# Earlier splits of transposed activations, a decay branch on ScalarE and a square summed by TensorE in a two-layer encoder

## The chip, the cores and the metric

The kernel runs on one NeuronCore of a Trainium2 chip. It is written in Python on a tile framework: each call becomes one instruction of an engine, and a scheduler sets the order of the instructions on each engine from the order in which they are written and from priorities. TensorE (PE; its weight loads are shown as PEld) multiplies, VectorE (DVE), ScalarE (ACT) and GpSimd (POOL) work elementwise, and SyncE's queue (SP) issues the transfers. Each engine takes its own instructions strictly in order. The metric is the device time of one execution in microseconds (us), the median over runs.

## The reference

The input is x, 512 tokens by 1024 features, float32. The trunk has two layers, each with a token mixer and a channel mixer, and each of these four stages is normalised before and after (a "sandwich"):

```python
for layer in range(DEPTH):                                   # DEPTH = 2
    hn = rms_norm(x, norm_mix_pre[layer])
    m = retention_na_mixer(hn, ...) if layer % 2 == 0 else ssd_mixer(hn, ...)
    x = x + rms_norm(m, norm_mix_post[layer])
    f = conv_geglu_ffn(rms_norm(x, norm_ffn_pre[layer]), ...)
    x = x + rms_norm(f, norm_ffn_post[layer])
```

The state space mixer (ssd_mixer) of the second layer is where two of the three edits are:

```python
proj = hn @ w_in                                             # z, x, B, C, dt
xbc = silu(depthwise_conv_centered(xbc, conv_w, conv_b))     # width 5
log_a = dt * A                                               # both directions
y = bidir_scan(C, B, xh * dt_f, xh * dt_b, log_a_f, log_a_b) # 4 groups of 8 heads, chunks of 128
y = (y + xh * d_skip) * silu(z)
yg = y * rsqrt(mean(y * y over the 512 features of a group) + EPS)
return (yg * norm_g) @ w_out
```

Within a chunk of the scan, position j takes from position l the product of C and B times a decay exp(cs_j - cs_l), where cs is the running sum of log_a: for l before j that of the forward direction, for l after j that of the backward one. The channel mixer is `u = conv3(hn @ w_up); (gelu(gate) * val) @ w_down` with 2816 inner features.

## The kernel before, in words

**Arithmetic.** Every large product is made of three matmuls (`mm3`, L84 to L88): a float32 operand is split into a rounded part "hi" and a rest "lo", and hi·hi (L86), lo·hi (L87) and hi·lo (L88) are summed in PSUM. `split` (L79) is two instructions, a cast on ACT (L81) that makes hi and a subtraction on DVE (L82) that makes lo. Weights arrive in units of 128 x 1024 (`wunit`: tile wst by DMA, then whi and wlo); activations are split as xh and xl (normalised input of a stage), yh and yl (output of the state space layer), hh and hl (inner features of the channel mixer).

**Between two stages** each of the four token tiles t goes through one chain: the last matmul of the tile gives m; mg = m·gain (L150); ACT sums the squares of m (junk, L119); v_m (DVE, L109) and r_m (POOL, L111) are the inverse root; x is updated in two halves (`post_norm`, L175); ACT sums the squares of x; v_x and r_x follow; xs, the normalised x, is made in two halves (`norm`, L131); PE transposes xs into pt (`turn`, L140); and `split` makes xh and xl of pt. Only then can the next stage multiply that tile. The splits of weights stand at `high_priority(60)`; that of `turn` has no raised priority. Tiles t2 and t3 at the end of a mixer are "late": their transposes are put between the first products of the next stage (`flush`). The channel mixer makes its first two feature tiles in two column halves, first the 256 columns of t0 and t1, then those of t2 and t3; the weights of the second feature tile go into buffers hh and hl of the channel mixer's own pool.

**The state space layer** works through 4 groups of 8 heads, by the order lists `SLOTS` (a letter each: t and n project a feature tile, h makes the decay matrix of a head, s a state, i the part between chunks, p a pair of heads, r the norm, o the output product of the group before, S and N the silus). `head` (from L730) fetches two rows broadcast over the partitions (pb[0] and pb[1], of 3 buffers, issued by SP), and for each of 4 chunks makes one branch with ACT (L741), takes the maximum with the other by one DVE instruction (L742), and makes ds with ACT (L744); then come an exponential on ACT (L745) and two products on DVE (L746, L747). `inter` starts y with x·d (L768, L769) and adds the parts between chunks. `pair` multiplies (py, L782), adds and gates (L785, L786), and takes the square sq on ACT (L788); POOL adds the squares of pairs 1 to 3 to that of pair 0 (L792), and then yh and yl are made (L794, L795). `rms` (L798) sums the added squares over partitions with four matmuls of one column (pss, L802), and DVE (ss, L804) and POOL (rg, L806) make the inverse root. After group 3 follows its output product with weights whi, wlo and wo, m (L828), and the chain between the stages.

## Time and profile before

| | before |
|---|---|
| median of 3 runs | 1434.11 us (1434.01 to 1434.52) |
| the profiled execution's own time | 1435.78 us |
| its span, first to last instruction | 1434.0 us |
| mean granted TensorE clock | 0.996 of full speed |
| PE busy | 1398.5 us (98%) |
| DVE busy | 946.3 us (66%) |
| ACT busy | 720.3 us (50%) |
| POOL busy | 60.6 us (4%) |

The profile is one execution taken by the hardware profiler. The table's shares are means over four stages: mixer 0, the first channel mixer, the state space layer (from about 620 us to about 1060 us), and the second channel mixer. An engine with a low mean can be full in one of them. The chain that ended last is made of PE for 80% of the span, of DVE for 9%, of ACT for 5%, and of transfers for 3%.

### The profile page before, as it was taken

How to read it: one execution, taken by the hardware profiler on the slowest of the kernel's cores; microseconds unless marked ns; L12 is line 12 of the kernel's file. 1: busy time of each engine (PE TensorE's matmuls, PEld its weight loads, DVE VectorE, ACT ScalarE, POOL GpSimd, SP SyncE). 2: the span in 40 equal slices, each digit the busy share in tenths (PEclk: the TensorE clock that was granted, in tenths of full speed). 3: DMA queues.
4: the chain of work that ended last, by engine and by line, in shares of the span. 5: the costliest groups of instructions: out<-in, count | busy, mean ns of one | idle time of the engine just before them, and what ended most of it. 6: DMA issues, size and time to landing. Idle time of an engine off the chain costs nothing.

```text
span 1434.0 us, 18009 instructions
## 1 busy us (share of the span) xinstructions
PE 1398.5 (98%) x6832; PEld 1141.0 (80%) x6832; DVE 946.3 (66%) x1486; ACT 720.3 (50%) x1192; POOL 60.6 (4%) x67
## 2 busy tenths in 40 slices
PE   7999999999999999999999999999889999999998
PEld 6877777898888888888777787777678888888886
DVE  7368888666566552357889786999886666564242
ACT  5356665454444431334888766577544444443230
POOL 0010110100000000000000000000110000000000
PEclk9999999999999999999999999999999999999999
DMA  7443232233233333332556354345432233333241
GB/s 255 146 141 92 85 96 77 83 108 102 89 98 95 102 94 97 120 107 95 159 180 184 111 176 131 95 153 162 143 120 87 90 100 94 100 89 102 89 132 59
DMA packets 56950, 166.34 MB, mean 116 GB/s; under 512 B 7200, under 2 KB 7968, under 8 KB 56864
## 3 DMA queue, kind: packets, MB, share of 16 engines
q1 hardware_dynamic: 56864, 165.20, 37.2%
q8 instruction: 54, 0.88, 0.2%
q14 instruction: 32, 0.26, 0.1%
HBM read 157.57 MB, written 5.51 MB: 114 GB/s over the span
## 4 chain that ended last, share of the span: by engine, by line
PE 80%; DVE 9%; ACT 5%; DMA 3%; issue 2%; POOL 0%; SPq 0%; DVEq 0%; POOLq 0%; ACTq 0%
PE mm L86 24%; PE mm L87 24%; PE mm L88 24%; DMA pb<-pd 1%; DVE wlo L82 1%; PE st L719 1%; DVE xf L683 1%; PE pt L140 1%; PE y L449 1%; PE pi L762 1%; DMA wst<-in_c_out 1%; PE pt L663 1%; PE py L782 1%; DVE ti L766 1%; DVE yl L795 0%
## 5 line engine op out<-in xcount | busy, mean ns | idle before, releaser
L88 PE MATMUL mm<-xl,whi 128*128 128x512 f32 (+2 forms) x1216 | 463.9, 382 | 4.0 <-DVE xl L82 3.8
L86 PE MATMUL mm<-xh,whi 128*128 128x512 f32 (+2 forms) x1216 | 464.0, 382 | 1.5 <-ACT z L689 0.7
L87 PE MATMUL mm<-xh,wlo 128*128 128x512 f32 (+2 forms) x1216 | 463.4, 381 | 1.4 <-DVE wlo L82 1.4
L82 DVE TENSOR_TENSOR wlo<-wst,whi 128x1024 fp32r<-128x1024 f32 (+1 forms) x208 | 255.5, 1229 | 198.0 <-ACT whi L81 195.8
L81 ACT CAST whi<-wst 128x1024 fp32r<-128x1024 f32 (+1 forms) x208 | 217.3, 1045 | 191.4 <-PE mm L87 119.6
L88 PEld LDWEIGHTS mm<-xl,whi 128*128 128x128 f32 (+1 forms) x1216 | 228.6, 188 | 48.4 <-DVE xl L82 4.5
L86 PEld LDWEIGHTS mm<-xh,whi 128*128 128x128 f32 (+1 forms) x1216 | 229.0, 188 | 46.8 <-issue 2.4
L87 PEld LDWEIGHTS mm<-xh,wlo 128*128 128x128 f32 (+1 forms) x1216 | 229.0, 188 | 45.2 <-DVE wlo L82 2.7
L227 DVE SCALAR_TENSOR_TENSOR cv<-mm,cwt,cv 128x511 f32<-128x511 f32 x88 | 65.7, 747 | 95.2 <-ACT cv L226 94.9
L86 PE MATMUL mm<-whi,hh 128*128 128x512 f32 x288 | 112.0, 389 | 0.0
L87 PE MATMUL mm<-whi,hl 128*128 128x512 f32 x288 | 112.0, 389 | 0.0
L88 PE MATMUL mm<-wlo,hh 128*128 128x512 f32 x288 | 112.0, 389 | 0.0
L226 ACT ACTIVATE cv<-mm,cwt 128x512 f32<-128x512 f32 x88 | 68.4, 777 | 39.8 <-PE mm L88 39.8
L81 ACT CAST hh<-cv 128x512 fp32r<-128x512 f32 x44 | 27.3, 621 | 100.5 <-DVE cv L235 100.3
L233 ACT ACTIVATE cv<-cv 128x512 f32<-128x512 f32 x44 | 27.8, 633 | 85.2 <-DVE cv L228 85.2
L228 DVE SCALAR_TENSOR_TENSOR cv<-mm,cwt,cv 128x511 f32<-128x511 f32 x88 | 66.0, 750 | 3.0
L744 ACT ACTIVATE ds<-um,tok,ddt 128x128 f32<-128x128 f32 x128 | 55.7, 484 | 16.1 <-DVE e L747 15.7
L88 PEld LDWEIGHTS mm<-wlo,hh 128*128 128x128 f32 x288 | 54.1, 188 | 11.3
L87 PEld LDWEIGHTS mm<-whi,hl 128*128 128x128 f32 x288 | 54.1, 188 | 11.2
L86 PEld LDWEIGHTS mm<-whi,hh 128*128 128x128 f32 x288 | 54.1, 188 | 11.2
L82 DVE TENSOR_TENSOR hl<-cv,hh 128x512 fp32r<-128x512 f32 x44 | 30.5, 693 | 28.9 <-ACT hh L81 28.9
L741 ACT ACTIVATE e<-pb,tok 128x128 f32<-128x128 f32 x128 | 43.0, 392 | 11.7 <-DMA pb<-pd 10.2
(236 smaller groups left out, 1945.6 us busy)
## 6 DMA issues: line engine op xcount, KB each, us to landing
wst<-in_f_up SPq DMA_DIRECT2D x88, 512.0 KB
wst<-in_f_down SPq DMA_DIRECT2D x44, 512.0 KB
wst<-in_c_fm SPq DMA_DIRECT2D x40, 512.0 KB
pb<-pd SPq DMA_DIRECT2D x64, 256.0 KB
wst<-in_ab_fm SPq DMA_DIRECT2D x20, 512.0 KB
gain<-yd SPq DMA_DIRECT2D x32, 256.0 KB
wst<-in_c_out SPq DMA_DIRECT2D x16, 512.0 KB
gain<-in_norms SPq DMA_DIRECT2D x8, 512.0 KB
```

Source lines behind the costliest of these rows:

```text
L81: self.nc.scalar.copy(hi, src)
L82: self.nc.vector.tensor_tensor(lo, src, hi.bitcast(F32), op=ALU.subtract)
L86: mm(out, lh, rh, start=first, stop=False)
L87: mm(out, ll, rh, start=False, stop=False)
L88: mm(out, lh, rl, start=False, stop=last)
L140: nc.tensor.transpose(pt[:, j], xs[:, j * P:(j + 1) * P], self.ident)
L226: nc.scalar.activation(o, ps, AF.Identity, scale=w(1), bias=w(3))
L227: nc.vector.scalar_tensor_tensor(o[:, 1:], ps[:, :S - 1], w(0), o[:, 1:], op0=ALU.mult, op1=ALU.add)
L228: nc.vector.scalar_tensor_tensor(o[:, :S - 1], ps[:, 1:], w(2), o[:, :S - 1], op0=ALU.mult, op1=ALU.add)
L233: nc.scalar.activation(g, g, AF.Gelu_apprx_tanh)
L741: nc.scalar.activation(e[:, c], pb[0][:, cc], AF.Identity, scale=-1.0, bias=tok[:, 0, c, h:h + 1])
L744: nc.scalar.activation(ds[:, c], um, AF.Identity, scale=ddt[:, c, h:h + 1], bias=tok[:, 1, c, H + h:H + h + 1])
```

## The change

There are three edits. In `turn`, the split of each transposed tile is put at `high_priority(100)`, above the weights' 60. In `head`, for the groups 2 and 3, the second branch is made by ACT in place in pb[1] (four instructions with a new bias ntok, the negated token column), and one DVE instruction of 128 x 512 takes the maximum; groups 0 and 1 stay as they were; in `inter`, the first 128 columns of x·d go from DVE to ACT in all groups. In `pair`, the square of pair 3 of groups 2 and 3 is no longer added by POOL; `rms` gives it to PE as a second operand, so that pss takes 8 one-column matmuls in these groups, each of which waits, by `together`, for all squares and additions from the third on.

```diff
@@ -139,7 +139,8 @@
             for j in range(4):
                 nc.tensor.transpose(pt[:, j], xs[:, j * P:(j + 1) * P], self.ident)
             o = (slice(None), slice(h * 4, h * 4 + 4), slice(t * P, (t + 1) * P))
-            self.split(self.xh[o], self.xl[o], pt)
+            with self.tc.high_priority(100):
+                self.split(self.xh[o], self.xl[o], pt)
 
     def post_half(self, st, t, n, ps, g_post, eng=None, m=None):
 
@@ -580,6 +581,7 @@
 
         tok = one.tile([P, 3, NT, H2], F32, name="tok")
         ddt = one.tile([P, NT, H], F32, name="ddt")
+        ntok = one.tile([P, NT, H], F32, name="ntok")
         etot = one.tile([P, H2, NT], F32, name="etot")
         pd = E.dram.tile([H2, S], F32, name="pd")
         yd = E.dram.tile([H2, S], F32, name="yd")
@@ -650,6 +652,7 @@
                         nc.tensor.transpose(pt[:, c].rearrange("p i h -> p (i h)"), s[:, c * C:(c + 1) * C], E.ident)
                     nc.scalar.copy(tok[:, i].rearrange("p (i c) h -> p c i h", i=2), pt)
             nc.vector.tensor_tensor(ddt, tok[:, 1, :, :H], tok[:, 1, :, H:], op=ALU.subtract)
+            nc.vector.tensor_scalar(ntok, tok[:, 0, :, H:], -1.0, None, op0=ALU.mult)
 
         def rows(i, dr, g, c):
             o = dr * H + g * HPG
@@ -739,9 +742,14 @@
             for c in range(NT):
                 cc = slice(c * C, (c + 1) * C)
                 nc.scalar.activation(e[:, c], pb[0][:, cc], AF.Identity, scale=-1.0, bias=tok[:, 0, c, h:h + 1])
-                nc.vector.scalar_tensor_tensor(e[:, c], pb[1][:, cc], tok[:, 0, c, H + h:H + h + 1], e[:, c],
-                                               op0=ALU.subtract, op1=ALU.max)
+                if g < 2:
+                    nc.vector.scalar_tensor_tensor(e[:, c], pb[1][:, cc], tok[:, 0, c, H + h:H + h + 1], e[:, c],
+                                                   op0=ALU.subtract, op1=ALU.max)
+                else:
+                    nc.scalar.activation(pb[1][:, cc], pb[1][:, cc], AF.Identity, bias=ntok[:, c, h:h + 1])
                 nc.scalar.activation(ds[:, c], um, AF.Identity, scale=ddt[:, c, h:h + 1], bias=tok[:, 1, c, H + h:H + h + 1])
+            if g >= 2:
+                nc.vector.tensor_tensor(e, e, pb[1].rearrange("p (c l) -> p c l", c=NT), op=ALU.max)
             nc.scalar.activation(e, e, AF.Exp, scale=-1.0)
             nc.vector.tensor_tensor(e, e, o["gt"], op=ALU.mult)
             o["m"][j] = e, nc.vector.tensor_tensor(e, e, ds, op=ALU.mult)
@@ -765,7 +773,7 @@
                 ti = E.tmp.tile([P, 384], F32, name="ti", tag="tmp")
                 nc.vector.tensor_tensor(ti, pi.rearrange("p c l -> p (c l)"), ysc[:, dr, cc], op=ALU.mult)
                 if dr == 0:
-                    nc.vector.tensor_scalar(y[:, :C], x[:, :C], d, None, op0=ALU.mult)
+                    nc.scalar.activation(y[:, :C], x[:, :C], AF.Copy, scale=d)
                     nc.vector.scalar_tensor_tensor(y[:, cc], x[:, cc], d, ti, op0=ALU.mult, op1=ALU.add)
                 else:
                     nc.vector.tensor_tensor(y[:, cc], y[:, cc], ti, op=ALU.add)
@@ -785,11 +793,14 @@
             nc.vector.tensor_tensor(y, py, y, op=ALU.add)
             nc.vector.tensor_tensor(y, y, o["t"][6 + q], op=ALU.mult)
             sq = (last if q == 0 else E.tmp).tile([P, S], F32, name="sq", tag="ssq" if q == 0 else "tmp")
-            nc.scalar.activation(sq, y, AF.Square)
+            w = nc.scalar.activation(sq, y, AF.Square)
             if q == 0:
-                o["sq"] = sq
+                o["sq"] = [sq]
+            elif q == 3 and o["g"] >= 2:
+                o["sq"].append(sq)
             else:
-                nc.gpsimd.tensor_tensor(o["sq"], o["sq"], sq, op=ALU.add)
+                w = nc.gpsimd.tensor_tensor(o["sq"][0], o["sq"][0], sq, op=ALU.add)
+            o["sqw"].append(w)
             yh, yl = four.tile([P, S], R32, name="yh"), four.tile([P, S], R32, name="yl")
             nc.scalar.activation(yh, y, AF.Identity, scale=col[:, 1, f:f + 1])
             nc.vector.scalar_tensor_tensor(yl, y, col[:, 1, f:f + 1], yh.bitcast(F32), op0=ALU.mult, op1=ALU.subtract)
@@ -799,7 +810,9 @@
 
             pss = E.px.tile([P, NT], F32, name="pss", tag="px")
             for c in range(NT):
-                nc.tensor.matmul(pss[:, c:c + 1], o["sq"][:, c * C:(c + 1) * C], mean, start=True, stop=True)
+                for i, sq in enumerate(o["sq"]):
+                    E.together([nc.tensor.matmul(pss[:, c:c + 1], sq[:, c * C:(c + 1) * C], mean, start=i == 0,
+                                                 stop=sq is o["sq"][-1])], o["sqw"][2:])
             ss = few.tile([P, NT], F32, name="ss", bufs=2)
             nc.vector.tensor_scalar(ss, pss, EPS, None, op0=ALU.add)
             o["r"] = few.tile([P, NT], F32, name="rg", bufs=2)
@@ -834,7 +847,7 @@
             for t in range(NT):
                 out_tile(o, n, t, ws)
 
-        gs = [dict(g=g, t={}, st={}, m={}, yi={}, y=[], silu=[]) for g in range(NG)]
+        gs = [dict(g=g, t={}, st={}, m={}, yi={}, y=[], silu=[], sqw=[]) for g in range(NG)]
         def tiles(o, *ii):
             for i in ii:
                 project(o, i)
```

The priority moves instructions in every place where a tile is turned. At the start, DVE's order for the first two tiles was wlo, xl, xl (tile 0), wlo, xl, xl (tile 1); it is now xl, xl (tile 0), wlo, xl, xl (tile 1), wlo, and PE has its first product of tile 1 (L86) as third matmul of the start, between L87 and L88 of tile 0.

The first place shown is DVE in the passage from the state space layer to the second channel mixer, around the split of tile t1: xs are the halves of a normalised tile, m and mg the outputs of later tiles, x_97 the running activation, xl_99 the split of a transposed tile, wlo weights. Before, from the xs of t1 to the first xs of t2:

```order
L131 SCALAR_TENSOR_TENSOR xs_9037<-x_97,r_x_9035,gain_8969 128x512
L131 SCALAR_TENSOR_TENSOR xs_9039<-x_97,r_x_9035,gain_8969 128x512
L82 TENSOR_TENSOR wlo_9211<-wst_9208,whi_9210 128x1024
L109 TENSOR_SCALAR v_m_9083<-ssm0_9058,ssm1_9079 128x1
L828 SCALAR_TENSOR_TENSOR m_9127<-mm_9114,rg_8945,x_97 128x512
L175 SCALAR_TENSOR_TENSOR x_97<-mg_9057,r_m_9085,x_97 128x512
L175 SCALAR_TENSOR_TENSOR x_97<-mg_9078,r_m_9085,x_97 128x512
L150 TENSOR_TENSOR mg_9130<-m_9127,gain_8881 128x512
L828 SCALAR_TENSOR_TENSOR m_9148<-mm_9135,rg_8945,x_97 128x512
L109 TENSOR_SCALAR v_x_9092<-ssx_9089 128x1
L82 TENSOR_TENSOR xl_99<-pt_9173,xh_98 128x4x128
L131 SCALAR_TENSOR_TENSOR xs_9096<-x_97,r_x_9094,gain_8969 128x512
```

and now, from the xs of t1 to the first xs of t2:

```order
L131 SCALAR_TENSOR_TENSOR xs_9061<-x_97,r_x_9059,gain_8993 128x512
L131 SCALAR_TENSOR_TENSOR xs_9063<-x_97,r_x_9059,gain_8993 128x512
L151 TENSOR_TENSOR mg_9154<-m_9151,gain_8901 128x512
L841 SCALAR_TENSOR_TENSOR m_9172<-mm_9159,rg_8969,x_97 128x512
L82 TENSOR_TENSOR xl_99<-pt_9197,xh_98 128x4x128
L82 TENSOR_TENSOR xl_99<-pt_9204,xh_98 128x4x128
L109 TENSOR_SCALAR v_m_9107<-ssm0_9082,ssm1_9103 128x1
L151 TENSOR_TENSOR mg_9175<-m_9172,gain_8901 128x512
L176 SCALAR_TENSOR_TENSOR x_97<-mg_9081,r_m_9109,x_97 128x512
L176 SCALAR_TENSOR_TENSOR x_97<-mg_9102,r_m_9109,x_97 128x512
L109 TENSOR_SCALAR v_x_9116<-ssx_9113 128x1
L131 SCALAR_TENSOR_TENSOR xs_9120<-x_97,r_x_9118,gain_8993 128x512
```

The two xl of t1 (the rows with xl_99) now stand together and ahead of the x of t2, where one of them stood behind it; the wlo, which stood behind the xs of t1, has gone ahead of them (it is now three rows above the first row shown), and the products m and mg of t3 have gone ahead of the x of t2.

The second place is DVE a little later, from the xs of t2 to the subtraction hl of the second feature tile's weights. Before:

```order
L131 SCALAR_TENSOR_TENSOR xs_9098<-x_97,r_x_9094,gain_8969 128x512
L150 TENSOR_TENSOR mg_9151<-m_9148,gain_8881 128x512
L82 TENSOR_TENSOR xl_99<-pt_9180,xh_98 128x4x128
L109 TENSOR_SCALAR v_m_9156<-ssm0_9131,ssm1_9152 128x1
L175 SCALAR_TENSOR_TENSOR x_97<-mg_9130,r_m_9158,x_97 128x512
L175 SCALAR_TENSOR_TENSOR x_97<-mg_9151,r_m_9158,x_97 128x512
L82 TENSOR_TENSOR hl_9216<-wst_9218,hh_9214 128x512
L82 TENSOR_TENSOR hl_9217<-wst_9218,hh_9215 128x512
L82 TENSOR_TENSOR hl_9226<-wst_9228,hh_9224 128x512
```

and now:

```order
L131 SCALAR_TENSOR_TENSOR xs_9122<-x_97,r_x_9118,gain_8993 128x512
L109 TENSOR_SCALAR v_m_9180<-ssm0_9155,ssm1_9176 128x1
L176 SCALAR_TENSOR_TENSOR x_97<-mg_9154,r_m_9182,x_97 128x512
L82 TENSOR_TENSOR xl_99<-pt_9310,xh_98 128x4x128
L82 TENSOR_TENSOR xl_99<-pt_9317,xh_98 128x4x128
L176 SCALAR_TENSOR_TENSOR x_97<-mg_9175,r_m_9182,x_97 128x512
L82 TENSOR_TENSOR hl_9240<-wst_9242,hh_9238 128x512
L82 TENSOR_TENSOR hl_9241<-wst_9242,hh_9239 128x512
L82 TENSOR_TENSOR hl_9250<-wst_9252,hh_9248 128x512
```

The two xl of t2 have come between the two halves of the last x (that of t3), and ahead of the hl; before, they stood behind the hl, below the rows shown, and the second xl of t1 stood here instead.

The third place is PE at the sum of squares of the last group: sq are the squares, yh and yl the output of the pairs, whi and wo the weights of two 512-column halves. Before:

```order
L87 MATMUL mm_8925<-wo_8883,yl_8818 128x512
L86 MATMUL mm_8912<-whi_8892,yh_8877 128x512
L88 MATMUL mm_8925<-wo_8883,yh_8817 128x512
L86 MATMUL mm_8925<-wo_8883,yh_8877 128x512
L87 MATMUL mm_8912<-whi_8892,yl_8878 128x512
L88 MATMUL mm_8912<-wlo_8893,yh_8877 128x512
L87 MATMUL mm_8925<-wo_8883,yl_8878 128x512
L88 MATMUL mm_8925<-wo_8883,yh_8877 128x512
L802 MATMUL pss_8938<-mean_5190,sq_8701 128x1 x4
L87 MATMUL mm_8982<-whi_8892,yl_8818 128x512
```

and now:

```order
L86 MATMUL mm_8932<-whi_8912,yh_8836 128x512
L86 MATMUL mm_8945<-wo_8903,yh_8836 128x512
L86 MATMUL mm_9006<-whi_8912,yh_8836 128x512
L814 MATMUL pss_8958<-mean_5190,sq_8719 128x1
L814 MATMUL pss_8958<-mean_5190,sq_8895 128x1
L814 MATMUL pss_8958<-mean_5190,sq_8719 128x1
L814 MATMUL pss_8958<-mean_5190,sq_8895 128x1
L814 MATMUL pss_8958<-mean_5190,sq_8719 128x1
L814 MATMUL pss_8958<-mean_5190,sq_8895 128x1
L87 MATMUL mm_8932<-whi_8912,yl_8837 128x512
L88 MATMUL mm_8932<-wlo_8913,yh_8836 128x512
L86 MATMUL mm_8932<-whi_8912,yh_8897 128x512
```

Six of the eight one-column matmuls have moved ahead of every product with a lo part (yl) of pairs 2 and 3, which the four of before stood behind for the first two outputs; the other two stand ten matmuls further on.

## Rows read from the trace of the kernel before

**Rows 1.** the page's first part, whole span: busy us of each engine, share, instructions.

```profile
PE 1398.5 (98%) x6832; PEld 1141.0 (80%) x6832; DVE 946.3 (66%) x1486; ACT 720.3 (50%) x1192; POOL 60.6 (4%) x67
```

**Rows 2.** waits of TensorE, whole span: what waited for what: us, times, longest.

```profile
PE mm L88 <- DVE xl L82: 3.8, 1, 3.8
PE pss L802 <- POOL sq L792: 0.9, 1, 0.9
PE pt L663 <- ACT bf L689: 0.9, 1, 0.9
```

**Rows 3.** timeline of VectorE at the start (start us, us, line, out<-in, count).

```profile
11.13 1.22 DVE L82 TENSOR_TENSOR wlo<-wst,whi 128x1024 fp32r<-128x1024 f32 x1
12.26 1.28 DVE L82 TENSOR_TENSOR xl<-pt,xh 128x512 fp32r<-128x512 f32 x2
```

**Rows 4.** timeline of PE's matmuls and weight loads at the same place.

```profile
13.60 0.63 PE L88 MATMUL mm<-wlo,xh 128*128 128x512 f32 x1
13.00 0.29 PEld L87 LDWEIGHTS mm<-whi,xl 128*128 128x128 f32 x1 [0.51 <-DVE xl L82]
```

**Rows 5.** by form, 860 to 1045 us: count, busy us, mean ns, idle before.

```profile
L742 DVE SCALAR_TENSOR_TENSOR e<-pb,tok,e 128x128 f32<-128x128 f32 x52 | 15.2, 343 | 2.6 <-DMA pb<-pd 2.6
L746 DVE TENSOR_TENSOR e<-e,gt 128x512 f32<-128x512 f32 x16 | 10.7, 682 | 0.7 <-ACT e L745 0.7
L741 ACT ACTIVATE e<-pb,tok 128x128 f32<-128x128 f32 x52 | 16.7, 391 | 2.6 <-DMA pb<-pd 2.3 <-PE py L782 0.3
```

**Rows 6.** stretches: length, then busy us of PE, PEld, DVE, ACT, POOL; clock.

```profile
970.00:980.00 10.00, 10.00 (x53) 7.73 (x53) 7.92 (x19) 9.52 (x17) 0.50 (x1) 1.00 0.39 121
980.00:990.00 10.00, 10.00 (x41) 7.41 (x41) 10.00 (x16) 8.94 (x23) 0.00 (x0) 1.00 0.43 123
```

**Rows 7.** the stall at 1021 us, timelines of PE and ScalarE.

```profile
1025.40 1.09 PE L782 MATMUL py<-e,xt 128*64 128x128 f32 x16 [3.69 <-DVE ti L766]
1021.01 1.14 ACT L81 CAST wo<-wst 128x512 fp32r<-128x512 f32 x2 [1.39 <-DMA wst<-in_c_out]
```

**Rows 8.** squares of the last group: POOL, VectorE, PE; VectorE in group 2 last.

```profile
1035.77 3.36 POOL L792 TENSOR_TENSOR sq<-sq 128x512 f32<-128x512 f32 x2 [5.61 <-ACT sq L788]
1036.27 3.41 DVE L795 SCALAR_TENSOR_TENSOR yl<-y,col,yh 128x512 fp32r<-128x512 f32 x2
1040.77 0.95 PE L802 MATMUL pss<-mean,sq 128*128 128x1 f32 x8
926.53 1.41 DVE L795 SCALAR_TENSOR_TENSOR yl<-y,col,yh 128x512 fp32r<-128x512 f32 x2
```

**Rows 9.** VectorE from the layer's output to the next one, timeline.

```profile
1043.06 1.41 DVE L828 SCALAR_TENSOR_TENSOR m<-mm,rg,x 128x512 f32<-128x512 f32 x2 [1.14 <-POOL rg L806]
1056.85 1.41 DVE L131 SCALAR_TENSOR_TENSOR xs<-x,r_x,gain 128x512 f32<-128x512 f32 x2
1060.17 1.41 DVE L175 SCALAR_TENSOR_TENSOR x<-mg,r_m,x 128x512 f32<-128x512 f32 x2
1063.67 1.41 DVE L131 SCALAR_TENSOR_TENSOR xs<-x,r_x,gain 128x512 f32<-128x512 f32 x2
1067.06 1.41 DVE L175 SCALAR_TENSOR_TENSOR x<-mg,r_m,x 128x512 f32<-128x512 f32 x2 [0.65 <-POOL r_m L111]
1069.28 2.50 DVE L82 TENSOR_TENSOR hl<-wst,hh 128x512 fp32r<-128x512 f32 x4 [0.81 <-ACT hh L81]
```

**Rows 10.** PE and ScalarE in the same stretch, timelines.

```profile
1063.67 0.39 PE L88 MATMUL mm<-xl,whi 128*128 128x256 f32 x1 [3.83 <-DVE xl L82]
1068.63 2.18 ACT L81 CAST hh<-wst 128x512 fp32r<-128x512 f32 x4 [4.58 <-issue]
1078.30 0.28 PE L86 MATMUL mm<-xh,whi 128*128 128x256 f32 x1
```

**Rows 11.** stretches at two granted clocks, columns as in group 6.

```profile
1064.20:1067.50 3.30, 3.16 (x15) 2.87 (x14) 2.65 (x6) 0.00 (x0) 0.54 (x1) 0.50 0.30 89
1067.60:1071.00 3.40, 3.40 (x30) 3.40 (x30) 2.59 (x5) 2.37 (x5) 0.00 (x0) 1.00 0.38 143
```

## The prediction

> **What bounds the kernel now.** I read the page's first part: PE is busy for 98% of the span, DVE for 66%, ACT for 50% [rows 1]. So an instruction less on DVE or ACT is worth nothing by itself; only the places where PE stands still, or runs at half clock, can be won. The view of waits names those that bear on the change [rows 2]: one of 3.8 us for an xl of L82, one of 0.9 us for the added squares before pss, one of 0.9 us for a transposition behind ACT's bf, and smaller ones. One more, for ti, is the largest in the state space layer: 3.69 us [rows 7]. The view of stretches adds what a long wait does to the clock: after the wait for xl the granted clock is 0.50 for 3.3 us, in which 15 matmuls of 256 columns start, where the next stretch, at 1.00, has 30 in 3.4 us [rows 11]. So this stretch lost 3.3 / 2 = some 1.7 us.
>
> The sum below is made against the profiled execution, 1435.78 us with a span of 1434.0. The median of the runs is 1434.11, 1.67 lower; I carry the differences over to it. The runs shown lie within 0.5 us; a change within 0.2% (2.9 us) I call none.
>
> **The start.** PE waits 0.51 us for the xl of tile 0 [rows 4], since this stands on DVE behind a wlo of 1.22 us [rows 3]. With xl first it can begin at 11.13 and the wait goes. But L88 needs that wlo, which then ends at about 11.13 + 1.2 (the pair of xl, by the start-to-start time of the next row) + 1.22 = 13.55; L88 started at 13.60 anyway. What is won is the one matmul of tile 1 that PE now does between. A matmul there is shown with 0.63 us [rows 4], and starts overlap: between 0 and 0.6, I take -0.45.
>
> **The passage through groups 2 and 3.** Per head DVE loses four L742 of 0.343 us and gets one instruction of 128 x 512, for which L746 stands (0.682 us) [rows 5]: for 16 heads -22.0 + 10.9 = -11 us on DVE. ACT gets 64 instructions like L741, of 0.391 us [rows 5]: +25 us, and 16 of x·d. DVE's work is mostly hidden by PE already: in the fullest stretch, 980 to 990, DVE is busy for all of 10 us and PE still runs without a gap [rows 6]. So I credit half of the waits that hang on DVE's lateness (0.9 for bf and about as much in smaller ones: -0.8). In group 2 the wait of 0.9 before pss goes with POOL's last addition. Its price is four more one-column matmuls: the four of before take 0.8 us (8 records from 1040.77, 0.95 us with the overlap) [rows 8], so +0.8 for four more, -0.1 together. Sum -0.9. Bounds: -2.0, if all waits go, and +3.3, if ACT is late (the second rival).
>
> Here the Trainium skill speaks against the change: "Trainium Architecture — The Big Picture", section "The five engines, in one table", names simple arithmetic as what ScalarE is not for, VectorE being up to about three times as fast per element. By that an instruction on ACT could cost 3 x 0.343 = 1.03 us, an estimate, and 64 of them 41 us more than I count, and the second rival would be the forecast. This trace has 0.391 against 0.343 us for the same 128 x 128 tile, so the measurement decides against the rule at this size.
>
> **The stall at 1021 us** ends with DVE's ti, but DVE is not its cause: the wo casts on ACT wait for a transfer of weights, after which come a table load, the gate z, y and ti [rows 7]. That transfer waits for a weight buffer that PE's own products free. The change leaves this chain and its order as it was. I take 0, bounds -0.7 and +0.7 (the last head, now with more ACT work, stands just ahead of it).
>
> **The squares of the last group.** Before, POOL adds two squares for 3.36 us beside the two yl of DVE, which take 3.41 us together [rows 8], where a pair without POOL's work beside it took 1.41 [rows 8]. With one addition left, one yl should be slow and one quick, 1.7 + 0.7 = 2.4 us, 1.0 earlier. And two x·d of 0.28 us [rows 5] leave DVE's chain ahead of it, a gain of 0.4 with their overlap. Against that stand four more one-column matmuls, and six of the eight now stand ahead of the yl products, so that not all of the 1.4 arrives: 0.8 us of matmuls goes off. With a little of it lying in a wait, I take the first m of the output (at 1043.06 before [rows 9]) 0.75 us earlier; bounds 0.3 and 1.3.
>
> **The passage to the second channel mixer** is the largest term, and is bound by DVE, whose order changes. I lay DVE's new order out with the durations and start-to-start times of before, and count from the first m (T0). Before: xs of t1 at T0 + 13.8, first x of t2 at T0 + 17.1, xs of t2 at T0 + 20.6, PE's L88 from its 3.83 us wait at the same T0 + 20.6, the last x at T0 + 24.0, hh at T0 + 25.6, the second column half on PE at T0 + 35.2 [rows 9, 10].
> Now xs of t1 has a wlo (1.2) and one more m ahead, and ends up at T0 + 15.4. Its transposition comes 1.6 us later too, and PE, which reached it at T0 + 13.7, waits there. Then xl of t1 follows behind only an mg and an m: from T0 + 18.0, first half ready at 18.7. L88 can start 1.9 us earlier than before. But x of t2 has moved back: it starts at T0 + 20.0, and DVE has nothing to do until xs of t2, which follows the end of x by the chain of ACT, DVE and POOL; before, from the end of x at 1060.17 + 1.41 to xs at 1063.67, that chain took 2.1 us [rows 9], filled with other work, now it is idle time. xs of t2 is at 23.4. Then come the first half of x of t3, at 25.5, the two xl of t2 (1.25), and the second half, done at 28.1 instead of 25.4.
> The casts hh start only when that x is done, since their buffers are the mixer's until then; so hh moves from T0 + 25.6 to 28.2, hl follows by 0.6, and PE, which is sooner at the end of its first products, waits for them instead. xs of t3 comes at 32.4, its transposition at 33.1, and the second column half at T0 + 36.8: 1.6 us later than before. With T0 0.75 earlier that is +0.85. The half clock I leave as it is: one long wait is replaced by several shorter ones (about 2.4, 1.0 and 2 to 3 us), and I assume one stretch of 0.50 among them, as before. Bounds: -5.5, if the late hh costs PE nothing (first rival), and +0.85 + 1.7 = +2.5, if two stretches at half clock follow.
>
> The other places where tiles are turned (into the first channel mixer and into the state space layer) get their xl earlier too. No wait of PE for an xl is listed there (the one of 3.8 us is counted once [rows 2]), so 0.
>
> **Sum:** -0.45 - 0.9 + 0 + 0.85 (with the squares in it) = -0.5; 1434.11 - 0.5 = 1433.6. Its own range is 1431.5 to 1436.
>
> **Rivals.**
> First, faster: the wait for xl goes in full, with its half clock, and hh is not what PE waits for. That is -3.83 - 1.7 = -5.5, with the start and the groups -6.9: 1427.2. For it: this is the one long wait that the view names, and the change aims its two xl at it. Against it: the order of DVE puts x of t3 behind two more xl, and hh cannot start before it. Chance 0.25.
> Second, slower: ACT becomes late in group 2. From 970 to 990 it is busy for 9.52 + 8.94 of 20 us [rows 6]; one or two heads in each 10 us add 1.6 to 3.1 us each, 4.8 in all, which makes 23.3 of 20. Being in order, ACT would be 3.3 us late with the silus, the copies of transposed tiles and the casts of weights that stand behind. If PE waits for one of them in full, this costs 3.3, and the 0.8 credited to DVE's relief is gone: 1433.6 + 4.1 = 1437.7. It decides from the point at which ACT's backlog exceeds the lead of those casts over PE. Against it: DVE, whose maxima ACT's exponentials wait for, is relieved by the same edit. Chance 0.18.
> Third, within the forecast's own range: half clock after each of the two longer waits of the passage, 1435.3. That the clock falls after such waits is what the one wait of 3.83 us shows [rows 10, 11]. The Trainium skill ("TensorE: Matmul & The Clock Gate", section "What's actually happening") says that the clock is set by how busy TensorE has lately been; by that, several short waits close together may cost a second time as one long one does, and the trace has no such group of waits to show it.
>
> **How the numbers follow.** Forecast (with the third) 0.57, first rival 0.25, second 0.18. Faster by over 0.2% (below 1431.2): nearly all of the first and a twentieth of the forecast, 0.28. Slower (above 1437.0): three quarters of the second and 0.03 of the forecast, 0.17. Within: 0.55. The range that leaves one in ten out on either side goes from 1428.0, inside the first rival, to 1437.7, at the second.
>
> **What would show it.** In the new profile: no wait for xl at 13.0; DVE near 11 us less and ACT over 25 us more; a wait of over 3 us for ti still there; the first m 0.75 us earlier; the wait for xl in the passage down to about 1 us, with new ones before the transposition of t1 and at the first matmul with hh; the second column half 0.85 us later in all. The forecast is wrong if hh comes no later than before against the first m, if no wait stands at hh, or if waits for ACT of over 1 us stand between 960 and 1020.

## The result and the profile after

| | before | after |
|---|---|---|
| median (7 runs each) | 1434.11 us (1433.23 to 1436.95) | 1441.78 us (1437.32 to 1443.77) |
| ratio after to before | | 1.0047, 95% interval 1.0032 to 1.0062 |
| the profiled execution | 1435.78, span 1434.0 | 1443.77, span 1442.0 |
| mean granted clock of TensorE in it | 0.996 | 0.990 |

The change made the kernel slower by 7.7 us in the medians, and by 6.7 (4.6 to 8.9) by the ratio. The forecast was 1433.6, its range ended at 1437.7. The first part of the page of after (busy us and share of the span):

```profile
PE 1405.0 (97%) x6848; PEld 1147.5 (80%) x6848; DVE 935.1 (65%) x1423; ACT 744.9 (52%) x1272; POOL 57.2 (4%) x65
```

Against [rows 1], DVE has 11.2 us less work and ACT 24.6 more; the forecast had near 11 and over 25. What matters is PE's waits, the view of waits of after (us, times, longest):

```profile
PE py L790 <- DVE ti L774: 3.8, 1, 3.8
PE mm L86 <- ACT hh L81: 3.2, 1, 3.2
PE pt L666 <- ACT bf L692: 1.9, 1, 1.9
PE pss L814 <- POOL sq L802: 0.9, 1, 0.9
PE mm L88 <- DVE xl L82: 0.3, 1, 0.3
```

The wait for xl, 3.8 us in [rows 2], is down to 0.3, and the wait for ti at the stall is what it was [rows 7]. The 0.9 us for pss belong to an earlier group now, at 788 us; in group 2, where before had them, the wait is down to 0.3. New are 3.2 us at the first matmul with hh and 2.1 before the transposition of t1 (below), and the wait for bf in group 3 has doubled from 0.9 to 1.9. In or behind each of these three the clock falls to half. The stretches of after at 0.50 between 20 and 1400 us (length, then busy us of PE, PEld, DVE, ACT, POOL, then the clock, the share of the DMA engines and GB/s):

```profile
939.10:942.40 3.30, 3.30 (x21) 2.54 (x20) 3.30 (x6) 3.28 (x5) 0.00 (x0) 0.50 0.84 234
969.80:973.10 3.30, 3.30 (x10) 2.55 (x9) 2.27 (x3) 2.78 (x6) 1.88 (x1) 0.50 0.34 87
1027.80:1031.10 3.30, 1.56 (x16) 1.59 (x18) 2.55 (x5) 3.30 (x7) 0.00 (x0) 0.50 0.56 171
1031.20:1034.50 3.30, 3.18 (x22) 2.12 (x18) 3.30 (x4) 1.67 (x3) 2.27 (x1) 0.50 0.66 179
1065.40:1068.70 3.30, 3.03 (x14) 2.74 (x14) 2.87 (x6) 0.09 (x1) 0.92 (x1) 0.50 0.47 158
1075.60:1078.90 3.30, 1.91 (x7) 1.61 (x8) 2.48 (x5) 2.72 (x5) 0.00 (x0) 0.50 0.00 0
1079.00:1082.30 3.30, 3.30 (x18) 3.30 (x17) 1.89 (x4) 0.84 (x3) 0.54 (x1) 0.50 0.91 264
```

The reader is to see seven rows of 3.3 us at half clock: behind bf (939), behind the one-column matmuls of pss (970), at the stall and in its wake (1028 and 1031), behind the transposition of t1 (1065), and at hh (1076 and 1079). A clock of 0.50 is 1.2 GHz, the lower of its two levels. Before had two such stretches in all, one behind the stall and one behind xl [rows 11]. From 20 us to 1400 the granted clock is 0.50 for 6.8 us in before and for 23.9 in after.

The passage to the second channel mixer, DVE of after, as [rows 9] of before (start us, us, line, operation):

```profile
1046.84 1.41 DVE L841 SCALAR_TENSOR_TENSOR m<-mm,rg,x 128x512 f32<-128x512 f32 x2 [1.13 <-POOL rg L819]
1062.68 1.41 DVE L131 SCALAR_TENSOR_TENSOR xs<-x,r_x,gain 128x512 f32<-128x512 f32 x2
1065.27 1.28 DVE L82 TENSOR_TENSOR xl<-pt,xh 128x512 fp32r<-128x512 f32 x2
1067.71 1.42 DVE L176 SCALAR_TENSOR_TENSOR x<-mg,r_m,x 128x512 f32<-128x512 f32 x2 [0.43 <-POOL r_m L111]
1071.21 1.42 DVE L131 SCALAR_TENSOR_TENSOR xs<-x,r_x,gain 128x512 f32<-128x512 f32 x2 [0.66 <-POOL r_x L111]
1073.40 0.75 DVE L176 SCALAR_TENSOR_TENSOR x<-mg,r_m,x 128x512 f32<-128x512 f32 x1 [0.66 <-POOL r_m L111]
1074.07 1.28 DVE L82 TENSOR_TENSOR xl<-pt,xh 128x512 fp32r<-128x512 f32 x2
1075.27 0.74 DVE L176 SCALAR_TENSOR_TENSOR x<-mg,r_m,x 128x512 f32<-128x512 f32 x1
1076.83 2.50 DVE L82 TENSOR_TENSOR hl<-wst,hh 128x512 fp32r<-128x512 f32 x4 [0.82 <-ACT hh L81]
```

and PE and the casts hh, as [rows 10]:

```profile
1063.58 1.29 PE L140 MATMUL pt<-head,xs 128*128 128x128 f32 x8 [2.14 <-DVE xs L131]
1066.01 0.58 PE L88 MATMUL mm<-xl,whi 128*128 128x256 f32 x1 [0.27 <-DVE xl L82]
1076.85 0.58 PE L86 MATMUL mm<-xh,hh 128*128 128x256 f32 x1 [3.24 <-ACT hh L81]
1086.29 0.28 PE L86 MATMUL mm<-xh,whi 128*128 128x256 f32 x1
```
```profile
1076.18 2.18 ACT L81 CAST hh<-wst 128x512 fp32r<-128x512 f32 x4 [1.90 <-DVE x L176]
```

The first m (T0) is at 1046.84, the second column half (the last row of PE) at 1086.29: T0 + 39.4, where before had 1078.30 - 1043.06 = 35.2. The first m itself is 3.8 us later than before (1046.84 against 1043.06), so that of the 8.0 us by which the two spans differ 3.8 lie ahead of the passage and 4.2 in it. The order is the forecast one: xs of t1 at T0 + 15.8, both xl of t1 close behind it (before, both and not only one of them came after the x of t2, at 1062.93 and 1065.61), x of t2 later (20.9), DVE's idle stretch, xs of t2 (24.4), the two halves of the last x with the two xl of t2 between them (26.6 and 28.4), then hh at 29.3.

### The profile page after: what moved, and what is told of

It is laid out like the page before. It is cut to its first block, busy times and chain, and to the rows that moved or that the text cites. A ratio compares the mean times of both kernels' runs of the same rounds, so it can differ in the third digit from the quotient of the medians.

```text
span 1442.0 us, 18051 instructions
## 1 busy us (share of the span) xinstructions
PE 1405.0 (97%) x6848; PEld 1147.5 (80%) x6848; DVE 935.1 (65%) x1423; ACT 744.9 (52%) x1272; POOL 57.2 (4%) x65
## 3 DMA queue, kind: packets, MB, share of 16 engines
q1 hardware_dynamic: 56864, 165.20, 36.8%
## 4 chain that ended last, share of the span: by engine, by line
PE 79%; DVE 8%; ACT 6%; DMA 4%; issue 2%; POOL 0%; SPq 0%; DVEq 0%; POOLq 0%; ACTq 0%
PE mm L86 24%; PE mm L87 24%; PE mm L88 24%; DMA pb<-pd 2%; DVE wlo L82 1%; PE pt L140 1%; ACT e L744 1%; PE y L450 1%; ACT whi L81 1%; PE st L722 1%; PE pi L770 1%; DVE xf L686 1%; ACT ds L750 1%; PE py L790 1%; PE sc L434 0%
## 5 line engine op out<-in xcount | busy, mean ns | idle before, releaser
L86 PE MATMUL mm<-xh,whi 128*128 128x512 f32 (+2 forms) x1216 | 464.6, 382 | 0.7 <-ACT z L692 0.5
L87 PE MATMUL mm<-xh,wlo 128*128 128x512 f32 (+2 forms) x1216 | 463.4, 381 | 0.9 <-DVE wlo L82 0.9
L88 PE MATMUL mm<-xl,whi 128*128 128x512 f32 (+2 forms) x1216 | 463.7, 382 | 0.3 <-DVE xl L82 0.3
L81 ACT CAST whi<-wst 128x1024 fp32r<-128x1024 f32 (+1 forms) x208 | 217.3, 1045 | 185.4 <-PE mm L87 119.1
L86 PEld LDWEIGHTS mm<-xh,whi 128*128 128x128 f32 (+1 forms) x1216 | 229.0, 188 | 45.8 <-issue 1.7
L88 PEld LDWEIGHTS mm<-xl,whi 128*128 128x128 f32 (+1 forms) x1216 | 228.9, 188 | 44.7 <-issue 1.1
L87 PEld LDWEIGHTS mm<-xh,wlo 128*128 128x128 f32 (+1 forms) x1216 | 229.1, 188 | 44.3 <-DVE wlo L82 1.5
L86 PE MATMUL mm<-whi,hh 128*128 128x512 f32 x288 | 112.0, 389 | 0.0
L87 PE MATMUL mm<-whi,hl 128*128 128x512 f32 x288 | 112.0, 389 | 0.0
L88 PE MATMUL mm<-wlo,hh 128*128 128x512 f32 x288 | 112.0, 389 | 0.0
L87 PEld LDWEIGHTS mm<-whi,hl 128*128 128x128 f32 x288 | 54.1, 188 | 11.3
L86 PEld LDWEIGHTS mm<-whi,hh 128*128 128x128 f32 x288 | 54.1, 188 | 11.2
L88 PEld LDWEIGHTS mm<-wlo,hh 128*128 128x128 f32 x288 | 54.1, 188 | 11.1
L686 DVE SCALAR_TENSOR_TENSOR xf<-mm,cwt,xf 128x510 f32<-128x510 f32 (+1 forms) x64 | 47.3, 741 | 5.1 <-ACT xf L683 4.9
```

Of the source, the lines that this page charges most:

```text
L81: self.nc.scalar.copy(hi, src)
L86: mm(out, lh, rh, start=first, stop=False)
L87: mm(out, ll, rh, start=False, stop=False)
L88: mm(out, lh, rl, start=False, stop=last)
L686: nc.vector.scalar_tensor_tensor(r[:, a], ps[:, b], wc(j), r[:, a], op0=ALU.mult, op1=ALU.add)
```

## The experiments

Ratios are to the kernel before, run beside each kernel on the same chip. The fourth column is the start of the second column half on PE less that of the first m on DVE, from the same two rows as above; "waits" are PE's at hh and for bf in group 3.

| run | edits | ratio, 95% interval | passage, us | waits, us |
|---|---|---|---|---|
| before | | | 35.2 | none, 0.9 |
| changed kernel | all | 1.0047 (1.0032 to 1.0062) | 39.4 | 3.2, 1.9 |
| e12_changed | all, again | 1.0048 (1.0030 to 1.0066) | 38.3 | 3.4, 1.5 |
| e1_turn, e5_turn_look | turn | 1.0018 (1.0006 to 1.0030) | 38.6 | 3.4, 1.0 |
| e2_head, e15_head_look | decays, x·d | 1.0021 (1.0007 to 1.0034) | 35.9, 36.1 | none, 1.1 and 1.4 |
| e3_squares | squares | 0.9993 (0.9981 to 1.0004) | 35.4 | none, 1.5 |
| e4_no_turn | all but turn | 1.0009 (0.9999 to 1.0019) | 36.1 | none, 2.5 |
| e6_hh_free | all, hh free | 1.0024 (1.0014 to 1.0034) | 35.2 | 0.4, 2.6 |
| e7_fill | all, filled wait | 1.0029 (1.0017 to 1.0042) | 37.9 | none, 2.2 |
| e8_combo | turn, squares, hh free | 0.9993 (0.9984 to 1.0002) | 34.9 | 0.4, 0.5 |
| e9_best | e8 with two orders | 1.0019 (1.0008 to 1.0030) | 35.7 | 0.7, 0.2 |
| e10_bf_hh | all, hh free, bf first | 1.0015 (1.0007 to 1.0023) | 35.2 | 0.4, 0.6 |
| e11_head_bf | decays, x·d, bf first | 1.0023 (1.0013 to 1.0033) | 35.5 | none, 0.2 |
| e13_branch | decays | 1.0042 (1.0027 to 1.0056) | 36.5 | none, 3.5 |
| e14_xd | x·d | 1.0031 (1.0019 to 1.0043) | 38.8 | none, 0.9 |

**Each edit alone, and all but one.** The theory (A) was that the passage loses it; the rivals were the groups, by ACT (B1) or by pss (B2). e1 is before with

```diff
-            self.split(self.xh[o], self.xl[o], pt)
+            with self.tc.high_priority(100):
+                self.split(self.xh[o], self.xl[o], pt)
```

> Only the edit in turn (splits of transposed tiles first); groups, decays and squares as before. Theory A (the order of VectorE in the passage to the second channel mixer makes the casts hh late, and TensorE then runs at half clock): start -0.9, wait at the first matmul with hh of 2 to 3 us with 0.50 clock after it, in all +3 to +5 us against before, 1437 to 1439. Rival B (the loss comes from the groups: pss and the waits behind ScalarE): the passage alone costs nothing or gains, 1431 to 1434. Only A predicts a wait of over 2 us at hh.

Measured: 1.0018, some 2.6 us (0.9 to 4.3), a little under what A expected (3 to 5). The traced execution is a further one (e5):

> The edit in turn alone once more, for a look at an undisturbed execution. Theory A: in the passage to the second channel mixer the wait for xl (3.8 us before) falls under 0.5 us, one of about 2 us stands before the transposition of t1 and one of over 2.5 us at the first matmul with hh, granted clock 0.50 behind it; the passage costs 3 us more than before. Rival B: no wait of over 1 us at hh.

Its wait at hh, in the view of waits:

```profile
PE mm L86 <- ACT hh L81: 3.4, 1, 3.4
```

The passage is 3.4 us longer than before, as A said. But this execution took 1443.9 us, and its span is 8.0 us longer than that of before: the other 4.6 lie ahead of the first m (1047.69). Two waits there are followed by half clock, at 88.8 and at 764.7 us:

```profile
88.07 0.50 PE L87 MATMUL mm<-xh,wlo 128*128 128x512 f32 x1 [1.19 <-DVE wlo L82]
763.65 0.66 PE L664 MATMUL pt<-head,bf 128*128 128x128 f32 x4 [2.16 <-ACT bf L693]
```

The twelve runs of e1 have a median of 1438.6, and the first of the two waits also stands in e11, which has not got the edit; so these 4.6 us are not shown to be its price. e2 is before with the edits in `head` and `inter`, here cut to two places:

```diff
-                nc.vector.scalar_tensor_tensor(e[:, c], pb[1][:, cc], tok[...], e[:, c], ...)
+                if g < 2:
...
+                else:
+                    nc.scalar.activation(pb[1][:, cc], pb[1][:, cc], AF.Identity, bias=ntok[:, c, h:h + 1])
...
-                    nc.vector.tensor_scalar(y[:, :C], x[:, :C], d, None, op0=ALU.mult)
+                    nc.scalar.activation(y[:, :C], x[:, :C], AF.Copy, scale=d)
```

> Only the second decay branch and x*d on ScalarE; order of the splits and squares as before. Theory A: within 1 us of before, 1433 to 1435. Rival B1 (ScalarE is the loss: bf comes late in group 3's first products and the clock falls to 0.50 behind that wait): the wait before the transposition of bf at about 938 us grows from 0.9 to 1.5 us or more, half clock follows at 939, +2 to +4 us, 1436 to 1438.

Measured: 1.0021, 3.0 us (1.0 to 4.9), against A. But its traced execution has a span of 1433.9, no longer than before, and a wait for bf of only 1.1. Of its 12 runs 5 have a mean granted clock of 0.991; of the 34 of before beside it none is under 0.993. e3 is before with the edit in `pair` and `rms` (cut to `pair`):

```diff
-                nc.gpsimd.tensor_tensor(o["sq"], o["sq"], sq, op=ALU.add)
+            elif q == 3 and o["g"] >= 2:
+                o["sq"].append(sq)
+            else:
+                w = nc.gpsimd.tensor_tensor(o["sq"][0], o["sq"][0], sq, op=ALU.add)
```

> Only the square of pair 3 given to TensorE in groups 2 and 3. Theory A: within 1 us of before. Rival B2 (the eight one-column matmuls of pss cost 0.9 us more each time and, being 1.9 us in which TensorE has nearly nothing to do, are followed by a stretch at half clock): granted clock 0.50 for 3.4 us behind pss of group 2 at about 970 us, +2 to +3.5 us there, and nothing won back in the last group, 1436 to 1438.

Measured: no difference, and no half clock behind pss in this execution; B2 falls as a cause by itself. e4 is the changed kernel with the split in `turn` as before:

> The changed kernel without the edit in turn: decay branch, x*d and squares changed, splits in their order of before. Theory A: most of the +7.7 us goes, 1434 to 1437, with the wait of 3.8 us for xl back and none at hh. Rivals B1 and B2: most of it stays, 1439 to 1443, with half clock behind bf (939 us) and behind pss (970 us).

Measured: 1.0009, which is 5.6 us less than the changed kernel run later (e12). Its waits for xl and bf:

```profile
PE mm L88 <- DVE xl L82: 3.8, 1, 3.8
PE pt L665 <- ACT bf L691: 2.5, 1, 2.5
```

So A holds for the larger part. What remains, 1.3 us, is not clear of noise; in this trace the longest new wait is the one for bf.

**What in the passage.** e6 takes away what makes hh wait: the first weight unit of the second feature tile goes into whi and wlo, whose buffers are not the mixer's. The line is in the function of both channel mixers, so that the edit reaches the first one too.

```diff
-        w0 = [[E.wunit(w_up[s, f], extra() if 2 * f + s >= 2 else None) for s in range(2)] for f in range(2)]
+        w0 = [[E.wunit(w_up[s, f], extra() if 2 * f + s >= 3 else None) for s in range(2)] for f in range(2)]
```

> The changed kernel, but the weights of the second feature tile's first half go into the ordinary weight buffers (whi, wlo) and not into the channel mixer's pool, so that their casts need not wait for the last x. Theory A (hh late is what the passage loses): no wait of over 1 us at those products, no half clock behind it, 3 to 6 us less than the changed kernel, ratio to before 1.0005 to 1.0025. Rival B (the loss is in the groups): ratio stays at 1.0035 to 1.006. Rival C (VectorE's order is late as a whole, the next thing it makes is late instead, xs of t3): the wait moves to the transposition of t3, and less than 2 us are won.

Measured: 1.0024, some 3.4 us less than the changed kernel, the passage 35.2. PE's timeline there, the transposition of t1 and the first matmul with the other hh:

```profile
1064.11 1.75 PE L140 MATMUL pt<-head,xs 128*128 128x128 f32 x8 [3.06 <-DVE xs L131]
1076.76 0.38 PE L86 MATMUL mm<-xh,hh 128*128 128x256 f32 x1 [0.38 <-ACT hh L81]
```

The wait at hh has gone, and one before the transposition of t1 is 3.1 where it was 2.1, since DVE now makes this unit's wlo ahead of xs of t1; the passage is 4.2 and 3.1 us shorter than in the two traces of the changed kernel. A holds, C falls. In the first channel mixer the same edit costs something, a new wait before a transposition:

```profile
289.59 0.63 PE L140 MATMUL pt<-head,xs 128*128 128x128 f32 x4 [0.85 <-DVE xs L131]
```

It stands in all four kernels with hh free (0.7 to 1.2 us in e6, e8, e9 and e10) and is 0.2 us or nothing in the others, so that their ratios understate what the passage won by about 1 us. e7 fills the wait of the changed kernel with work that nothing reads:

```diff
+                if c == 0 and i == 1 and done.__name__ == "store":
+                    fill = E.px.tile([P, 256], F32, name="fill", tag="px")
+                    for k in range(28):
+                        E.nc.tensor.matmul(fill, w0[0][0][0][0][:, :P], E.xh[:, k % KD, :256], start=True, stop=True)
```

> The changed kernel with 28 more matmuls of 256 columns (28 x 0.12 = 3.4 us at full clock) on TensorE between the transposition of t2 and the first matmul with hh, where it waits 3.2 us; nothing reads them. If the clock is what makes the wait dear: granted clock 1.00 from there to the second column half, 24 products with hh in 2.9 us and not 5.1, 1.5 to 3 us less than the changed kernel, ratio to before 1.0028 to 1.004. If the wait alone is what costs: no gain, ratio 1.0045 to 1.006.

Its stretches at the products with hh (columns as above):

```profile
1077.30:1080.60 3.30, 2.86 (x22) 2.46 (x21) 2.48 (x5) 2.04 (x4) 0.00 (x0) 1.00 0.00 0
1080.60:1083.50 2.90, 2.61 (x22) 2.41 (x21) 2.12 (x5) 1.19 (x3) 0.55 (x1) 1.00 0.63 191
```

The clock stayed at 1.00 there, and the casts hh come as late as in after (T0 + 29.3). From hh to the second column half this trace takes 8.5 us, the changed kernel 10.1 and 9.5, so half clock at hh costs some 1.0 to 1.6 us. The passage is 37.9: the rest, 2.6 us over before, is there without it. So in the traces the clock is the smaller part of this loss, the late hh the larger. The ratio, 1.0029, is 2.7 us below that of the changed kernel, but the two intervals overlap, and by the runs alone the two parts can't be told apart.

**Combinations.** e8 is before with the edits of e1, e3 and e6.

> The edits in turn and in the squares with the weights of the second feature tile's first half in the ordinary buffers; decays and x*d as before. Theory A: the passage keeps what the early xl win and does not pay for hh: 2 to 6 us less than before, ratio 0.996 to 0.9985. Rival B: the turn's order costs in the passage anyway: ratio 0.999 to 1.002.

Measured: 0.9993 (0.9984 to 1.0002): not to be told from before, nor from e3. A's range is missed and B's holds: even with hh free no gain from the order of `turn` shows. It is some 7.9 us better than the changed kernel. It has the shortest passage, 34.9, but the wait that xl lost stands again before the transposition of t1 (3.7 us), and it pays at 290 us as e6 does. e9 adds to e8 a lower priority for that unit and the steps of bf first, as in e10:

```diff
+            up = {0: 60, 1: 60, 2: 30, 3: 60}
...
+                with tc.high_priority(100) if i == 0 and g == 3 else ExitStack():
+                    nc.vector.scalar_tensor_tensor(r[:, a], ps[:, b], wc(j), r[:, a], op0=ALU.mult, op1=ALU.add)
```

> Squares and turn as in the changed kernel, decays as before; weights of the second feature tile's first half in the ordinary buffers with a lower priority, so that their wlo fills VectorE's idle time behind the x of t2; the four convolution steps of bf in group 3 first on VectorE. By the mechanisms shown so far: wait before the transposition of t1 from 3.7 to about 2.5 us, none at hh, none over 0.3 us at bf: 3 to 6 us less than before, ratio 0.996 to 0.998. If the passage is bound by VectorE as a whole, whatever its order: 0.999 or more, like the combination without these two.

Measured: 1.0019, a miss, though the waits it aimed at did become small (bf 0.2, transposition of t1 2.4). It has a stretch at half clock at 968 us in its trace, which e8 has not. Why it is slower than e8 was not settled.

**What in the groups.** The trace of after shows how bf became late. ACT, DVE and PE around 938 us:

```profile
932.65 1.28 ACT L753 ACT_TABLE_LOAD   x1
936.79 1.28 ACT L692 ACT_TABLE_LOAD   x1
938.08 0.63 ACT L692 ACTIVATE bf<-bf 128x512 f32<-128x512 f32 x1
```
```profile
934.61 0.69 DVE L754 TENSOR_TENSOR e<-e,gt 128x512 f32<-128x512 f32 x1 [0.94 <-ACT e L753]
935.22 0.74 DVE L686 SCALAR_TENSOR_TENSOR bf<-mm,cwt,bf 128x510 f32<-128x510 f32 x1
```
```profile
938.77 0.91 PE L666 MATMUL pt<-head,bf 128*128 128x128 f32 x4 [1.92 <-ACT bf L692]
```

DVE's order has a head's product e·gt ahead of the last convolution step of bf; it waits 0.94 us for ACT's exponential, which stands behind a table load. Then ACT needs another table load before the silu of bf, and PE waits 1.92. e10 is e6 with the steps of bf put first (the last two lines of e9's diff), and e11 is e2 with the same.

> The changed kernel with hh's weights in the ordinary buffers, and with the four convolution steps of bf in group 3 put first on VectorE, so that they stand ahead of the decay's products, which wait for ScalarE. Theory D (the decay edit costs because it puts such products ahead of the last step of bf, TensorE waits 2 to 2.6 us for bf, and half clock follows): wait for bf under 0.5 us, clock 1.00 there, 2 to 3 us less than with hh alone freed, ratio 1.000 to 1.001. Rival E (ScalarE is simply too full with the added branch): the wait moves to the next user of ScalarE in the group, ratio stays at 1.002 or more.

> Only decays and x*d on ScalarE (as in the decay edit alone, ratio 1.0021), with the steps of bf in group 3 first. Theory D: the edit alone then costs nothing, ratio 0.999 to 1.000. Rival E: ratio 1.0015 to 1.003.

PE's transpositions of bf in e10, and in e11 with pss of group 2:

```profile
932.33 0.66 PE L666 MATMUL pt<-head,bf 128*128 128x128 f32 x4 [0.61 <-ACT bf L693]
```
```profile
935.46 0.66 PE L665 MATMUL pt<-head,bf 128*128 128x128 f32 x4 [0.17 <-ACT bf L692]
968.76 1.05 PE L810 MATMUL pss<-mean,sq 128*128 128x1 f32 x8 [2.01 <-POOL sq L800]
```

The wait for bf all but goes in both (0.6 and 0.2), and no half clock follows. But e10 is only 1.3 us better than e6 (1.0015 against 1.0024, and the intervals overlap), and e11 not better than e2: in e11 PE, sooner through bf, waits 2.0 us at pss for POOL, 0.9 in before. Theory D is right about the wait and wrong about the price. E's ratio came in e11; in e10 the ratio lies between the two. E's reason, ScalarE being too full, is not shown: the wait that came instead is one for POOL.

> The changed kernel once more, beside the others. Both theories: ratio to before 1.004 to 1.006. Its trace tells which waits and stretches at half clock recur: by theory D the ones behind bf (939 us) and at hh (1076 us) do, the one behind pss (970 us) need not.

The changed kernel again: 1.0048. But this traced execution has a span of 1435.4, where the first had 1442.0, with the same program and the same waits at hh and nearly so for bf:

```profile
PE mm L86 <- ACT hh L81: 3.4, 1, 3.4
PE pt L666 <- ACT bf L692: 1.5, 1, 1.5
```

Its granted clock is 0.50 for 10.2 us (from 20 us to 1400), not 23.9. The difference, 13.7 us at half pace, is worth up to 6.8; the spans differ by 6.6. The first m is at 1041.44 here, 1.6 us sooner than before where the first trace had it 3.8 later, and the passage is 3.1 us longer than before where it was 4.2: what recurs is the passage, and what differs lies mostly ahead of it.

Three more runs were to tell where the decay edit loses: e13 is e2 with x·d on DVE, e14 is before with x·d on ACT alone, e15 another execution of e2.

> Only the second decay branch of groups 2 and 3 on ScalarE; x*d stays on VectorE. If the branch is what the decay edit costs (ratio 1.0021 for both): 1.0015 to 1.003, with some runs at a mean clock of 0.992 or less. If x*d is: 0.999 to 1.0005.

> Only x*d of the first 128 columns on ScalarE, in all groups. If the branch is what the decay edit costs: 0.999 to 1.0005, no run below a mean clock of 0.993, as before. If x*d is: 1.0015 to 1.003.

> The decay edit alone, a second execution with a trace. If its loss lies in waits of group 2 and 3 that only sometimes pull the clock down: a wait of over 1 us for bf at 937 us or for pss at 966 us, and a stretch at 0.50 behind one of them, and the span 2 us or more above the 1433.9 of the first look. Otherwise a span within 1 us of it and half clock only behind the stall at 1025 us and the wait for xl.

Both halves have a higher ratio than the whole: 1.0042 and 1.0031 against 1.0021. Each interval overlaps that of the whole, but they do not add: 6.0 and 4.5 us for the halves, 3.0 for the whole. In each the order is another one, and other waits appear: in e13 for xf and bf, in e14 for the added squares before the last pss:

```profile
865.37 0.47 PE L86 MATMUL mm<-xh,whi 128*128 128x512 f32 x1 [2.89 <-DVE xf L685]
943.89 0.82 PE L665 MATMUL pt<-head,bf 128*128 128x128 f32 x4 [3.50 <-ACT bf L691]
```
```profile
1040.57 1.87 PE L802 MATMUL pss<-mean,sq 128*128 128x1 f32 x8 [2.03 <-POOL sq L792]
```

e14 also has a passage of 38.8 us, though nothing of it was edited. In e15 the span is 1434.0, and there is half clock behind pss at 966. So which half loses can't be said, and the 3 us of e2 in the median are not in either of its traces. This stays open.

## Why the prediction was wrong

**The start.** The step came as worked out. PE makes one matmul of tile 1 before L88:

```profile
12.78 0.63 PE L87 MATMUL mm<-whi,xl 128*128 128x512 f32 x1
13.21 0.63 PE L86 MATMUL mm<-whi,xh 128*128 128x512 f32 x1
13.64 0.63 PE L88 MATMUL mm<-wlo,xh 128*128 128x512 f32 x1
```

L88 starts at 13.64, 13.60 before [rows 4], behind one matmul more, which takes 0.43 us from start to start: some 0.4 us won, as forecast. After gained 1.0 us up to 20 us, but so did e3, whose order there is that of before: at 14.3 us both have matmuls of 0.39 us, before still 0.63. That is not the edit either way: e2 and e15 are one program, and their matmuls at this time are

```profile
14.26 0.63 PE L87 MATMUL mm<-whi,xl 128*128 128x512 f32 x1
14.24 0.39 PE L88 MATMUL mm<-wlo,xh 128*128 128x512 f32 x1
```

The pace rose earlier in some executions than in others, and the gain beyond 0.4 us is luck.

**The passage** is the step that failed in every trace: "the second column half at T0 + 36.8: 1.6 us later than before". It came at T0 + 39.4 and 38.3 in two executions of the changed kernel and at 38.6 with the edit in turn alone, 3.1 to 4.2 later. The mechanism was as described: hh is late because the last x is, and PE then waits there; e6 shows it, since without that wait the passage is that of before. Two sizes were wrong. First, the hand-laid chain has hh at 28.2; it came at 29.3, 28.8 and 29.1. In after xs of t1 is 0.4 us later than laid out, by a wait for a transfer of x and by pitches, and x of t2 0.9 later, 0.4 of it a wait for POOL's r_m. Second, from hh to the second column half the forecast has 8.6 us, and e7, at full clock, 8.5; but the changed kernel took 10.1 and 9.5 and the turn alone 9.5, since the products with hh ran at half clock. "I assume one stretch of 0.50 among them, as before" is where this went wrong: in the passage the three traces have a stretch behind the transposition of t1, as before had behind xl, and a second one at hh, in after of double length. That is the third rival, which the forecast named and left out of its sum.

**Ahead of the passage** the forecast has the first m 2.1 us earlier (0.45, 0.9 and 0.75). It came 1.6 earlier in one execution of the changed kernel (e12), and 3.8 later in the other, with three more stretches at half clock ahead of it: behind bf, behind pss and at the stall. The terms had no price for half clock in the groups at all.

**The groups.** The credit of 0.8 us for DVE's relief did not last: the relief came (11 us), and e2 and e4, whose start is that of before, turn bf of group 3 sooner than before (937.0 and 938.3 against 940.1) though they wait longer for it. Behind it most or all of that is lost: their first m is at 1042.4 and 1044.5, that of before at 1043.1. The forecast named ACT's lateness as a rival and put it at 970 to 990 us and at fullness; it came at 938, by the order of two table loads and one product. The price of pss was right: eight matmuls take 1.92 us, four 0.95 [rows 8], and the wait before it in group 2 is down to 0.3:

```profile
967.55 1.92 PE L814 MATMUL pss<-mean,sq 128*128 128x1 f32 x16 [0.29 <-issue]
```

The half clock that follows these matmuls in after was not priced.

**The squares of the last group.** In after the first m stands 17.3 us behind the py of the stall, 17.7 before: 0.4 us won, not 0.75. In e12 it is 17.3 too, with half clock no longer than before, and in e3, with this edit alone, 17.7. The yl are quicker, as laid out (1.99 us for two, 3.41 before [rows 8]), but ss waits for the last two of the eight matmuls, which start at 1045.01, 3.7 us behind the first six. The 0.28 us of x·d in this term are not among [rows 5]; the trace of before has 0.278 for them.

**The clock** over the whole program is the second error. The changed kernel has more waits of 1 to 4 us, and any of them may be followed by half clock in one execution and not in the next. Over all runs the mean granted clock is 0.9921 in the changed kernel (14 runs) and 0.9952 in before (the 30 beside e12): 0.0031 of 1440 us, some 4.5 us, more than any single term of the sum. It is an upper bound, since half clock costs nothing while PE waits, and the mean spans differ by some 6. For the turn edit alone it is 0.9941 against 0.9945, worth at most 0.6 us of its 2.6: there the late hh is the larger part. For the whole, turn, decays and squares alone add to 2.6 + 3.0 - 1.0 = 4.6 us, and 6.7 to 6.9 were measured, within the intervals. What the decay edit costs, and where, stays open.

## What to carry to other kernels

A wait that is taken from the page's list can come back at the next thing in the queue of the engine that ended it: before crediting it, lay that engine's new order out to the point where the bounding engine runs without waits again. An urgent instruction put ahead delays all that stands behind it, here the last x, which freed the buffers of the next weights. An experiment that edits a shared function changes every stage that calls it, as e6 did in the first channel mixer. And one profiled execution of a kernel with many short waits is a single draw (of the changed kernel the two traces are the slowest of seven runs and the fastest of seven): compare the granted clock of all runs before a trace is taken for the median.

## What the hardware showed that was not expected

Two executions of one program differ by 6.6 us of span, and the time at half clock is enough to account for it (23.9 and 10.2 us at 0.50). The length of a wait did not tell whether half clock follows it. For bf, waits of 1.9 to 3.5 us of PE were followed by it in after, e4, e5, e6, e7 and e13, and waits of 1.5 us or less in e3, e12 and e15 were not. But a wait of 2.0 us at pss in e11 was not followed by it, and one of 1.2 us for a wlo at 88 or 89 us was in e5 and e11, and was not in e7. In after, e6, e7 and e9 half clock also followed the 1.9 us of one-column matmuls of pss, before which PE had waited 0.3 us at most, while in e3, e4, e8, e10 and e12 the same matmuls were not followed by it.
